# Gate and up projections of a two-layer encoder as 2x2 block products with seven half-size products, one Trainium2 core

## The chip, the cores and the metric

The kernel runs on one core of one Trainium2 chip. The metric is the device time of one execution in microseconds (us); lower is better. The engines are TensorE (PE, with its weight loads as PEld), VectorE (DVE), ScalarE (ACT), GpSimd (POOL) and SyncE (SP), which issues all transfers from HBM.

## What is computed

Two layers, each of a token mixer and a SwiGLU channel mixer, over 512 frames of width 1024, and a final norm. The change touches the channel mixer alone:

```python
h2 = rms_norm(x, norm2_g[l])
x = x + (jax.nn.silu(h2 @ w_gate[l]) * (h2 @ w_up[l])) @ w_down[l]
```

with `w_gate` and `w_up` of 1024 x 2816 and `w_down` of 2816 x 1024, all float32.

## The kernel before

Everything is kept transposed: features lie on the 128 partitions, the 512 frames along the free dimension. A matrix block is 128 x 128 of weights against 128 x 512 of activations. To hold float32 accuracy each operand is split in a high part `hi` (a cast to float32r, on ACT) and a rest `lo` (the difference, on POOL or DVE), and each block product is three matmuls, hi·hi, hi·lo and lo·hi, issued by `mm3` (L327; the matmuls are L332 to L334).

Weights come in units. `loader` (L353) issues one transfer per unit, mostly 128 x 1024 numbers (four blocks of the contraction by two blocks of output columns, 512 KB), into one of four `raw` buffers. `halves` (L365) then makes the `hi` with one cast of 1024 numbers per partition (L368) and the `lo` with two subtractions of 512 (L373), into four `hi` and four `lo` buffers of 1024. A projection (`project`, L566) takes two units, 8 blocks of the contraction and 2 blocks (a pair) of 128 output columns, hence 8·2·3 = 48 matmuls of 512 columns into two banks of PSUM.

The channel mixer (`mixer`, L973) runs over 11 pairs, for each a gate projection and then an up projection, 22 projections in a layer. The right operand is `x` times the norm's gain, split once per layer by `norm_input` (L479); the norm's factor per frame (`nm2.rows`, from `norm_rstd`, L524) is multiplied in afterwards. After a gate projection each of the two 128 x 512 results goes through a multiplication by the rows (DVE), Silu (ACT) and another multiplication by the rows (POOL); after an up projection through a multiplication by the gate's result (DVE), a cast (ACT) and a subtraction (DVE, `split_lo`). `down` (L1006) then runs four projections over all 22 blocks of the activations; in the last layer the fourth is done in two halves of 256 frames.

No order of instructions is written by hand. Each piece is a generator that yields operations, and `Weave` (L60 on) plans them: it holds a clock per engine, a cost per operation, the buffers that are free, and one clock for the access that POOL and DVE share when both operands lie in SBUF. In `run` (L172) it takes the operation that can start first and, among those on the same engine that can start within a short horizon, the one of lowest rank. An operation with two possible engines goes to the one where it would end first; for DVE 2 us are added in that choice (`SHUN`), so that work goes to POOL unless it is far behind. What it picks is the program's order on each engine; every engine then works its queue in that order. Buffers for 128 x 512 results, `row()`, come from a pool of 66 that the planner does not count.

## Time and profile before

| | |
|---|---|
| median of 3 runs | 1153.08 us (1150.91 to 1153.38) |
| profiled execution, its own time | 1153.68 us |
| its span | 1151.2 us |
| PE, matmuls | 1139.3 us busy, 99%, 5306 recorded |
| DVE | 447.7 us busy, 39% |
| ACT | 403.9 us busy, 35% |
| POOL | 750.4 us busy, 65% |
| granted TensorE clock, mean | 0.997 of full speed |

A matmul's duration on the page is longer than the distance to the next one, because they are pipelined: the rate is read from the starts. The profiled execution is 2.5 us longer than its span, and 0.6 us above the median of the runs.

### The profile page before, as it was taken

The numbers are of one execution on the slowest core, as the hardware profiler recorded it, in microseconds if no ns is written. First come the engines' busy times: TensorE is split into PE (matmuls) and PEld (weight loads), VectorE is DVE, ScalarE is ACT, GpSimd is POOL, SyncE is SP. The second block draws the span as 40 slices with busy tenths as digits, with TensorE's granted clock in tenths as the row PEclk, the third lists the DMA queues.
The fourth block names the chain that finished last, engine by engine and source line by source line (L and its number), as shares of the span: only waits on it lengthen the run. The fifth ranks groups of instructions, "written<-read, shape, count | busy, mean of one in ns | idle before, by whom it ended". The sixth has DMA issues, their size and how long they took to land.

```text
span 1151.2 us, 13848 instructions
## 1 busy us (share of the span) xinstructions
PE 1139.3 (99%) x5306; PEld 953.4 (83%) x5306; DVE 447.7 (39%) x766; ACT 403.9 (35%) x531; POOL 750.4 (65%) x583
## 2 busy tenths in 40 slices
PE   8999999999999999999999999999999999999997
PEld 7888888888888888888888888888888888888897
DVE  4899873322222222111059997442222222210003
ACT  6324545332332323222232346452323323322241
POOL 5877977756655655555577699785655665654572
PEclk9999999999999999999999999999999999999999
DMA  9433122333333332323333312233333333323332
GB/s 283 114 105 92 37 78 87 92 110 92 92 105 97 110 100 93 122 98 99 97 103 97 94 60 67 70 112 94 92 94 103 96 92 97 105 83 101 101 121 82
DMA packets 118483, 114.11 MB, mean 99 GB/s; under 512 B 4113, under 2 KB 113809, under 8 KB 118417
## 3 DMA queue, kind: packets, MB, share of 16 engines
q1 hardware_dynamic: 118416, 113.23, 32.5%
q8 instruction: 41, 0.67, 0.2%
q14 instruction: 26, 0.20, 0.1%
HBM read 111.12 MB, written 2.10 MB: 98 GB/s over the span
## 4 chain that ended last, share of the span: by engine, by line
PE 80%; DVE 16%; DMA 1%; issue 1%; ACT 1%; POOL 0%; SPq 0%; DVEq 0%; ACTq 0%; POOLq 0%
PE acc L332 25%; PE acc L333 25%; PE acc L334 25%; DVE conv L308 11%; DVE big L301 4%; PE acc L459 1%; DVE big L308 1%; DMA x<-in_x_t 1%; PE acc L425 1%; PE conv L332 1%; PE conv L334 1%; PE conv L333 1%; DMA raw<-in_w_in 0%; ACT big L284 0%; DVE vmean L727 0%
## 5 line engine op out<-in xcount | busy, mean ns | idle before, releaser
L373 POOL TENSOR_TENSOR lo<-raw,hi 128x512 fp32r<-128x512 f32 x403 | 529.0, 1330 | 330.4 <-ACT hi L368 325.6
L332 PE MATMUL acc<-big,hi 128*128 128x512 f32 (+1 forms) x1516 | 584.2, 385 | 0.5 <-ACT big L284 0.4
L333 PE MATMUL acc<-big,hi 128*128 128x512 f32 (+1 forms) x1516 | 581.4, 383 | 0.3 <-DVE big L308 0.3
L334 PE MATMUL acc<-big,lo 128*128 128x512 f32 (+1 forms) x1516 | 581.2, 383 | 0.0
L368 ACT ACTIVATE hi<-raw 128x1024 fp32r<-128x1024 f32 (+1 forms) x208 | 214.6, 1033 | 506.8 <-PE acc L333 433.7
L333 PEld LDWEIGHTS acc<-big,hi 128*128 128x128 f32 x1516 | 285.4, 188 | 56.4 <-DVE big L308 1.1
L332 PEld LDWEIGHTS acc<-big,hi 128*128 128x128 f32 x1516 | 285.3, 188 | 56.3 <-ACT big L284 1.0
L334 PEld LDWEIGHTS acc<-big,lo 128*128 128x128 f32 x1516 | 285.3, 188 | 56.2
L301 DVE TENSOR_TENSOR big<-acc,big 128x512 f32<-128x512 f32 (+2 forms) x200 | 128.8, 656 | 356.9 <-PE acc L334 343.6
L301 POOL TENSOR_TENSOR big<-big,big 128x512 f32<-128x512 f32 (+2 forms) x176 | 227.6, 1306 | 50.5 <-ACT big L284 38.5
L284 ACT ACTIVATE big<-big 128x512 fp32r<-128x512 f32 (+2 forms) x176 | 106.8, 616 | 158.4 <-DVE big L301 136.3
L308 DVE SCALAR_TENSOR_TENSOR conv<-big,small,conv 128x482 f32<-128x482 f32 (+25 forms) x232 | 156.0, 729 | 4.0 <-ACT conv L284 2.9
L301 DVE TENSOR_TENSOR x<-acc,x 128x512 f32<-128x512 f32 (+1 forms) x30 | 19.6, 654 | 245.5 <-PE acc L334 245.4
L301 DVE TENSOR_TENSOR big<-big,big 128x512 fp32r<-128x512 f32 (+1 forms) x54 | 54.0, 1002 | 32.4 <-ACT big L284 32.4
L308 DVE SCALAR_TENSOR_TENSOR big<-x,small,big 128x512 fp32r<-128x512 f32 x32 | 32.8, 1036 | 18.9 <-ACT big L284 18.9
L284 ACT ACTIVATE big<-x,small 128x512 fp32r<-128x512 f32 (+1 forms) x48 | 29.8, 643 | 20.6 <-DVE x L301 19.1
L284 ACT ACTIVATE big<-x 128x512 f32<-128x512 f32 (+1 forms) x41 | 24.2, 597 | 14.6 <-DVE x L301 14.6
L332 PE MATMUL acc<-hi,big 128*128 128x512 f32 x64 | 24.9, 389 | 0.0
L333 PE MATMUL acc<-lo,big 128*128 128x512 f32 x64 | 24.9, 389 | 0.0
L334 PE MATMUL acc<-hi,big 128*128 128x512 f32 x64 | 24.9, 389 | 0.0
L332 PE MATMUL acc<-big,big 128*128 128x512 f32 (+1 forms) x64 | 21.4, 334 | 2.2 <-DVE y L308 1.4
L333 PE MATMUL acc<-big,big 128*128 128x512 f32 (+1 forms) x64 | 20.6, 322 | 0.0
(55 smaller groups left out, 333.7 us busy)
## 6 DMA issues: line engine op xcount, KB each, us to landing
raw<-in_w_down SPq DMA_DIRECT2D x45, 512.0 KB, 3.4
raw<-in_w_gate SPq DMA_DIRECT2D x44, 512.0 KB, 3.8
raw<-in_w_up SPq DMA_DIRECT2D x44, 512.0 KB, 3.8
raw<-in_w_in SPq DMA_DIRECT2D x32, 512.0 KB, 3.7
raw<-in_w_out SPq DMA_DIRECT2D x16, 512.0 KB, 3.4
raw<-in_w_in SPq DMA_DIRECT2D x28, 256.0 KB, 3.3
raw<-in_w_down SPq DMA_DIRECT2D x9, 256.0 KB, 2.6
x<-in_x_t SPq DMA_DIRECT2D x8, 256.0 KB, 4.5
```

The lines of the kernel that those rows point to most:

```text
L284: ACT.activation(out=t if out is None else out, in_=in_, func=func, **kw)
L301: name, cost, lambda eng=eng: eng.tensor_tensor(out=out, in0=in0, in1=in1, op=op),
L308: [("DVE", cost, lambda: DVE.scalar_tensor_tensor(out=out, in0=in0, scalar=scalar, in1=in1, op0=op0, op1=op1))],
L332: PE.matmul(o, lh, rh, start=start, stop=False)
L333: PE.matmul(o, lh, rl, start=False, stop=False)
L334: PE.matmul(o, ll, rh, start=False, stop=stop)
L368: lambda t: ACT.activation(out=t[:, 0:n], in_=raw[:, 0:n], func=AF.Copy))],
L373: engines[eng].tensor_tensor(out=t[:, a:b], in0=raw[:, a:b], in1=hi[:, a:b].bitcast(F32), op=ALU.subtract)
L425: PE.matmul(o[:, i:i + 1], src[:, t * P:(t + 1) * P], over[n], start=first and i == 0, stop=last and i == len(blocks) - 1, skip_group_chec ...
L459: PE.matmul(ps[:, t * P:(t + 1) * P], cols[:, t:t + 1].broadcast_to([P, P]), ident, start=True, stop=True,)
```

## The change

The first two pairs of each layer (`PLAIN = 2`) stay as they are. For the other nine, each projection is seen as a 2x2 block product: the weights A (1024 x 256) are cut in two halves of the contraction and two blocks of output columns, the normed input B in the same halves of the contraction and two halves of 256 frames. In place of eight half-size products there are seven, of sums and differences of the blocks (`winograd`). Each is 4 blocks of the contraction by three matmuls of 256 columns, 12 matmuls; a projection has 84 of 256 columns where it had 48 of 512.

- **Left factors** (`factors`): from a projection's two `raw` buffers, four sums S1 to S4 of 128 x 512 (`sums`), and then for each of A11, S1, S2, A12, S3, S4, A22 a cast (ACT) and a subtraction of 512. Both may go to POOL or DVE, without the 2 us for DVE (`shun` 0.0). Plain units too are now cast in pieces of 512. There are 11 `hi` and 11 `lo` buffers of 512 in place of four and four of 1024.
- **Right factors** (`right_factors`), once per layer, planned beside the plain pairs: for each of four k, the two halves' `x` times gain times rows (DVE), four sums of 256, and the splits of B11 (256), T1|T2, B21|B22 and T3|N4 (512 each); they stay in 28 rows until the last product. The row pool has 60 buffers in place of 66.
- **Banks.** The seven products use three banks X, Y, Z of 256 columns: X takes A11·B11, then S2·T2, S3·T3 and A22·N4 on top; Y takes S1·T1 and S4·B22; Z takes A12·B21. Between the steps the partial sums are read off: three copies on ACT (p1, p5, u2) and three additions on DVE (c11, c22, c12), each of 256 columns. A product that goes on adding to a bank waits until the sum in it has been read.
- **After them**, a gate's result goes through Silu alone (one of 512, two of 256, ACT); the up's is multiplied by it (one of 512, two of 256). The multiplications by the rows are gone. The splits of these 18 activations (cast and subtraction) are put off until the layer's last such product has been issued, that is beside the first `down`.

```diff
+HALVES = 11
+PLAIN = 2
...
-    big = ctx.enter_context(tc.tile_pool(name="big", bufs=66))
+    big = ctx.enter_context(tc.tile_pool(name="big", bufs=60))
...
-    wv.pool("hi", 4, lambda: named(wts, [P, 1024], F32R, "hi"))
-    wv.pool("lo", 4, lambda: named(wts, [P, 1024], F32R, "lo"))
+    wv.pool("sum", 2, lambda: named(wts, [P, 1024], F32, "sum", 2))
+    wv.pool("hi", HALVES, lambda: named(wts, [P, SEQ], F32R, "hi", HALVES))
+    wv.pool("lo", HALVES, lambda: named(wts, [P, SEQ], F32R, "lo", HALVES))
...
+    def halves(u, raw, n):
+        his = []
+        for a in range(0, n, SEQ):
+            src = raw[:, a:a + SEQ]
+            his.append((src, (yield cast(src, [raw]))))
+        for src, hi in his:
+            lo = yield rest_of(src, hi, [raw])
+            u.hi_t.append(hi)
+            u.lo_t.append(lo)
...
+    def factors(f, rank):
+
+        r0, r1 = f.raws
+        v0, v1 = (r.rearrange("p (a b) -> p a b", a=4) for r in f.raws)
+        a11, a21 = v0[:, :, 0:P], v0[:, :, P:2 * P]
+        a12, a22 = v1[:, :, 0:P], v1[:, :, P:2 * P]
+        src = {"A11": (a11, [r0]), "A12": (a12, [r1]), "A22": (a22, [r1])}
...
+            t = yield add(None, a21, a22, ALU.add, [r0, r1], ("sum", 1))
+            slots.append(t)
+            s1, s2 = (shaped(t[:, i * SEQ:(i + 1) * SEQ], a11) for i in range(2))
+            src["S1"] = s1, [t]
+            yield add(s2, s1, a11, ALU.subtract, [t, r0])
+            src["S2"] = s2, [t]
+            t = yield add(None, a11, a21, ALU.subtract, [r0], ("sum", 1))
+            slots.append(t)
+            s3, s4 = (shaped(t[:, i * SEQ:(i + 1) * SEQ], a11) for i in range(2))
+            src["S3"] = s3, [t]
+            yield add(s4, a12, s2, ALU.subtract, [slots[0], r1])
+            src["S4"] = s4, [t]
...
+        def factor(i, name):
+            yield lambda: turn[0] == i and name in src
+            a, reads = src[name]
+
+            def issue(t):
+                ACT.activation(out=shaped(t, a), in_=a, func=AF.Copy)
+
+            hi = yield Op([("ACT", 0.05 + 0.00094 * SEQ, issue)], reads, [], ("hi", 1))
+            turn[0] += 1
+            lo = yield rest_of(a, hi, reads, 0.0)
+            f.q[name] = hi, lo
...
+        fast_left = [2 * (KF // 2 - PLAIN)]
+        right = {n: [None] * 4 for n in ("B11", "T1", "T2", "B21", "T3", "B22", "N4")}
...
+            def prepare(k):
+                xa, xb, t, d = row(), row(), row(), row()
+                for x, m in ((xa, k), (xb, k + 4)):
+                    yield stt(x, xs[m], scol(l, S_N2 + m), nm2.rows, ALU.mult, ALU.mult)
+                if k % 2 == 0:
+                    pairs[k // 2] = row(F32R), row(F32R)
+                c = h1 if k % 2 else h0
+                ah, al = (a[:, c] for a in pairs[k // 2])
+                yield act(ah, xa[:, h0], AF.Copy)
+                yield split_lo(al, xa[:, h0], ah, "POOL/DVE", 0.0)
+                right["B11"][k] = ah, al
+                yield tt(t[:, h0], xa[:, h1], xa[:, h0], ALU.subtract, "POOL/DVE", 0.0)
+                yield tt(t[:, h1], xb[:, h1], t[:, h0], ALU.subtract, "POOL/DVE", 0.0)
+                yield tt(d[:, h0], xb[:, h1], xa[:, h1], ALU.subtract, "POOL/DVE", 0.0)
+                yield tt(d[:, h1], xb[:, h0], t[:, h1], ALU.subtract, "POOL/DVE", 0.0)
+                for x, n0, n1 in ((t, "T1", "T2"), (xb, "B21", "B22"), (d, "T3", "N4")):
+                    hi, lo = row(F32R), row(F32R)
+                    yield act(hi, x, AF.Copy)
+                    yield split_lo(lo, x, hi, "POOL/DVE", 0.0)
+                    right[n0][k] = hi[:, h0], lo[:, h0]
+                    right[n1][k] = hi[:, h1], lo[:, h1]
+
+            for k in range(4):
+                wv.spawn(prepare(k), base + 10.0 * 2 * PLAIN - 15.0 + 0.01 * k)
...
+            def add(out, x, name, last):
+                yield tt(out, banks[x][:, h0], out, ALU.add)
+                if last:
+                    wv.free("acc", banks[x])
+                done.add(name)
...
+                steps = (
+                    ("A11", "B11", "X", None, lambda: copy(a[:, h0], "X", "p1")),
+                    ("S1", "T1", "Y", None, lambda: copy(b[:, h1], "Y", "p5")),
+                    ("S2", "T2", "X", "p1", lambda: copy(a[:, h1], "X", "u2")),
+                    ("A12", "B21", "Z", None, lambda: add(a[:, h0], "Z", "c11", True)),
+                    ("S3", "T3", "X", "u2", lambda: add(b[:, h1], "X", "c22", False)),
+                    ("S4", "B22", "Y", "p5", lambda: add(a[:, h1], "Y", "c12", True)),
+                    ("A22", "N4", "X", "c22", None),
+                )
...
+                for n, (ln, rn, x, need, then) in enumerate(steps):
+                    yield lambda: ln in f.q
+                    lh, ll = f.q[ln]
+                    yield lambda: need is None or need in done
+                    names = [] if need is None else [
+                        f"{need}_of_{(b if need == 'p5' else a).tensor.name}"]
+                    if need == "c22":
+                        names = [b]
+                    for k in range(4):
+                        yield lambda: right[rn][k] is not None
+                        c = slice(k * P, (k + 1) * P)
+                        m = (lh[:, c], ll[:, c]) + right[rn][k]
+                        if x not in banks:
+                            banks[x] = yield mm3(
+                                None, *m, True, False, ("acc", 1), lambda p: p[:, h0], loose=True,
+                            )
+                        else:
+                            yield mm3(banks[x][:, h0], *m, False, k == 3, after=names, loose=True)
+                    wv.free("hi", lh)
+                    wv.free("lo", ll)
+                    if then:
+                        wv.spawn(then(), r + 1 + 0.1 * n)
+                    else:
+                        done.add("c21")
+                fast_left[0] -= 1
...
+            def gated(a, b, banks, done):
+                def one(need, part, out, src):
+                    yield lambda: need <= done
+                    yield act(out, src(), AF.Silu)
...
+                wv.spawn(one({"c11", "c12"}, "t0", a, lambda: a), 0.0)
+                wv.spawn(one({"c22"}, "c22", b[:, h1], lambda: b[:, h1]), 0.0)
+                wv.spawn(one({"c21"}, "c21", b[:, h0], lambda: banks["X"][:, h0]), 0.0)
...
+                    yield tt(out, src(), by(), ALU.mult, on, 0.0)
...
+                def split(t, x, need):
+                    yield lambda: need <= parts and not fast_left[0]
+                    hi, lo = row(F32R), row(F32R)
+                    yield act(hi, x, AF.Copy)
+                    yield split_lo(lo, x, hi, "POOL/DVE", 0.0)
+                    acts[2 * i + t] = hi, lo
+
+                for t, x, need in ((0, a, {"t0"}), (1, b, {"c22", "c21"})):
+                    wv.spawn(split(t, x, need), base + 10.0 * KF - 12.0 + 0.1 * i)
...
+            winograd(w_gate[l], i, gated)
+            winograd(w_up[l], i, lifted)
...
+        base = 10.0 * len(mains)
+        side.append((len(mains), right_factors, base))
         for i in range(KF // 2):
-            mixer(i)
+            if i < PLAIN:
+                mixer(i)
+            else:
+                fast_mixer(i)
```

**What moves on DVE, in the nine later pairs.** Before, one pair had six rows on DVE (the names: `acc` is PSUM, `big` a row of 128 x 512 in SBUF):

```order
L301 TENSOR_TENSOR big_455_2335<-acc_448_2283,big_445_2263 128x512 [waits PE_49,Pool_49]
L301 TENSOR_TENSOR big_457_2342<-big_455_2335,big_456_2341 128x512 [waits Activation_49]
L301 TENSOR_TENSOR big_459_2356<-acc_449_2284,big_447_2282 128x512 [waits PE_49,Pool_49]
L301 TENSOR_TENSOR big_464_2366<-big_459_2356,big_463_2365 128x512 [waits Activation_49]
L301 TENSOR_TENSOR big_469_2411<-acc_460_2357,big_421_2122 128x512 [waits PE_49]
L301 TENSOR_TENSOR big_471_2430<-acc_461_2358,big_421_2122 128x512 [waits PE_49]
```

Now, in the middle of layer 0's nine pairs, from the end of one up projection (`big_638`, `big_639` are its results, `acc_822`, `acc_832` and `acc_826` its banks X, Z and Y) into the factors of the next projections:

```order
L412 TENSOR_TENSOR lo_831_3900<-sum_819_3839,hi_830_3891 128x512 [waits PE_49,Activation_49]
L412 TENSOR_TENSOR lo_834_3918<-sum_819_3839,hi_833_3909 128x512 [waits PE_49,Activation_49]
L329 TENSOR_TENSOR big_638_2810<-acc_832_3905,big_638_2810 128x256 [waits PE_49]
L412 TENSOR_TENSOR lo_836_3935<-raw_792_3674,hi_835_3926 128x512 [waits Activation_49]
L329 TENSOR_TENSOR big_639_2811<-acc_822_3848,big_639_2811 128x256 [waits PE_49]
L329 TENSOR_TENSOR big_639_2811<-big_639_2811,big_592_2575 128x256 [waits DVE_49]
L457 TENSOR_TENSOR sum_840_3957<-raw_814_3801,raw_815_3810 128x512 [waits DMAHW4_49]
L329 TENSOR_TENSOR big_638_2810<-acc_826_3868,big_638_2810 128x256 [waits PE_49]
L329 TENSOR_TENSOR big_638_2810<-big_638_2810,big_591_2574 128x512 [waits DVE_49]
L457 TENSOR_TENSOR sum_840_3957<-sum_840_3957,raw_814_3801 128x512
L329 TENSOR_TENSOR big_639_2811<-acc_822_3848,big_592_2575 128x256 [waits PE_49]
L457 TENSOR_TENSOR sum_844_3992<-raw_814_3801 128x512
```

The subtractions for `lo`, which were POOL's (L373), and the sums stand on DVE, 11 to a projection, and the additions that read the banks stand between them. POOL has no row left in this stretch but three of the `sum` rows.

**What the first product waits for on DVE.** In layer 0, the last right factor (`big_598`) and then the left factors of the first projection of the new kind (before, DVE had at this place only the rows of the plain pairs, six to a pair, as shown above):

```order
L329 TENSOR_TENSOR big_598_2587<-big_527_2278,big_597_2586 128x512 [waits PE_49,Activation_49]
L412 TENSOR_TENSOR lo_599_2599<-sum_508_2253,hi_549_2370 128x512
L412 TENSOR_TENSOR lo_600_2602<-sum_508_2253,hi_552_2378 128x512
L412 TENSOR_TENSOR lo_602_2611<-raw_503_2224,hi_561_2422 128x512
L412 TENSOR_TENSOR lo_603_2616<-sum_536_2311,hi_564_2432 128x512
L412 TENSOR_TENSOR lo_604_2625<-sum_536_2311,hi_571_2473 128x512
L412 TENSOR_TENSOR lo_605_2633<-raw_503_2224,hi_576_2486 128x512
L329 TENSOR_TENSOR big_588_2551<-acc_574_2479,big_565_2446 128x512 [waits PE_49,Pool_49]
L329 TENSOR_TENSOR big_608_2642<-big_588_2551,big_607_2641 128x512 [waits Activation_49]
```

Six of the seven `lo` of the first new projection stand behind all right factors, and the multiplication that ends pair 1 (`big_588`) stands behind them.

**A hand-over of a bank on PE.** The end of S4·B22 (bank Y, `acc_868`) and the start of A22·N4 (bank X, `acc_864`):

```order
L362 MATMUL acc_868_4136<-big_584_2530,hi_854_4043 128x256
L363 MATMUL acc_868_4136<-big_585_2531,hi_854_4043 128x256
L364 MATMUL acc_868_4136<-big_584_2530,lo_855_4052 128x256
L362 MATMUL acc_868_4136<-big_594_2578,hi_854_4043 128x256
L363 MATMUL acc_868_4136<-big_595_2579,hi_854_4043 128x256
L364 MATMUL acc_868_4136<-big_594_2578,lo_855_4052 128x256
L362 MATMUL acc_864_4116<-big_562_2425,hi_856_4060 128x256 [waits DVE_49]
L363 MATMUL acc_864_4116<-big_563_2426,hi_856_4060 128x256
L364 MATMUL acc_864_4116<-big_562_2425,lo_857_4069 128x256
```

The first matmul of A22·N4 waits for DVE's addition c22, which reads X after S3·T3; the product S4·B22, 12 matmuls, stands between. S2·T2, S3·T3 and S4·B22 wait in the same way for copies on ACT, each with one product between.

## Rows read from the trace of the kernel before

**Rows 1.** The page: busy time by engine; TensorE's granted clock in 40 slices.

```profile
PE 1139.3 (99%) x5306; PEld 953.4 (83%) x5306; DVE 447.7 (39%) x766; ACT 403.9 (35%) x531; POOL 750.4 (65%) x583
PEclk9999999999999999999999999999999999999999
```

**Rows 2.** The page: the chain that ended last, by engine.

```profile
PE 80%; DVE 16%; DMA 1%; issue 1%; ACT 1%; POOL 0%; SPq 0%; DVEq 0%; ACTq 0%; POOLq 0%
```

**Rows 3.** TensorE in order of time, 1094 to 1112 us: start, duration, instruction.

```profile
1094.64 0.39 PE L332 MATMUL acc<-big,hi 128*128 128x512 f32 x1
...
1105.30 0.39 PE L334 MATMUL acc<-big,lo 128*128 128x512 f32 x1
1105.53 0.28 PE L332 MATMUL acc<-big,hi 128*128 128x256 f32 x1
...
1111.28 0.28 PE L332 MATMUL acc<-big,hi 128*128 128x256 f32 x1
```

**Rows 4.** Groups by line and form, DVE, ACT, POOL: count, busy us, mean ns, idle before.

```profile
L301 DVE TENSOR_TENSOR big<-acc,big 128x512 f32<-128x512 f32 x144 | 99.0, 690 | 356.5 <-PE acc L334 343.6 <-ACT big L284 9.7 <-PE acc L459 2.4
L301 DVE TENSOR_TENSOR big<-big,big 128x512 fp32r<-128x512 f32 x44 | 45.2, 1026 | 32.0 <-ACT big L284 32.0
L301 DVE TENSOR_TENSOR big<-acc,big 128x256 f32<-128x256 f32 x8 | 3.3, 413 | 0.0
L368 ACT ACTIVATE hi<-raw 128x512 fp32r<-128x512 f32 x13 | 8.2, 633 | 36.5 <-PE acc L333 30.4 <-PE acc L334 4.0 <-DMA raw<-in_w_in 1.8
L284 ACT ACTIVATE big<-big 128x512 f32<-128x512 f32 x68 | 42.5, 626 | 64.3 <-DVE big L301 64.2
L284 ACT ACTIVATE big<-x,small 128x256 f32<-128x256 f32 x16 | 7.1, 494 | 0.0
L284 ACT ACTIVATE big<-big 128x256 fp32r<-128x256 f32 x8 | 3.3, 410 | 0.6 <-DVE big L301 0.5
L373 POOL TENSOR_TENSOR lo<-raw,hi 128x512 fp32r<-128x512 f32 x403 | 529.0, 1330 | 330.4 <-ACT hi L368 325.6 <-issue 3.7 <-POOL big L301 0.6
```

**Rows 5.** Busy us of each engine (instructions) in two stretches, clock, DMA share, GB/s.

```profile
224.20:256.90 32.70, 32.70 (x146) 27.07 (x145) 7.50 (x10) 10.45 (x13) 20.71 (x16) 1.00 0.33 93
256.90:452.80 195.90, 195.90 (x866) 162.22 (x865) 43.41 (x55) 58.91 (x72) 118.26 (x90) 1.00 0.33 99
```

**Rows 6.** DVE in order of time, first mixers of layer 0, then the last.

```profile
224.22 1.32 DVE L301 TENSOR_TENSOR big<-acc,big 128x512 f32<-128x512 f32 x2 [4.20 <-PE acc L334]
233.08 0.69 DVE L301 TENSOR_TENSOR big<-acc,big 128x512 f32<-128x512 f32 x1 [7.54 <-PE acc L334]
234.47 0.69 DVE L301 TENSOR_TENSOR big<-big,big 128x512 fp32r<-128x512 f32 x1 [0.70 <-ACT big L284]
...
257.56 0.69 DVE L301 TENSOR_TENSOR big<-acc,big 128x512 f32<-128x512 f32 x1 [0.64 <-PE acc L334]
259.01 1.36 DVE L301 TENSOR_TENSOR big<-big,big 128x512 fp32r<-128x512 f32 x1 [0.76 <-ACT big L284]
...
453.40 0.69 DVE L301 TENSOR_TENSOR big<-acc,big 128x512 f32<-128x512 f32 x1 [0.64 <-PE acc L334]
```

**Rows 7.** POOL in order of time, 253 to 262 us.

```profile
253.10 2.55 POOL L373 TENSOR_TENSOR lo<-raw,hi 128x512 fp32r<-128x512 f32 x2 [1.66 <-ACT hi L368]
258.54 2.98 POOL L373 TENSOR_TENSOR lo<-raw,hi 128x512 fp32r<-128x512 f32 x2 [2.89 <-ACT hi L368]
```

**Rows 8.** The chain in order of time: start, length, what (pieces on DVE, one on ACT).

```profile
18.83 1.06 ACT hi L368
...
48.04 8.91 DVE conv L308 x14
...
593.47 0.74 DVE conv L308
594.23 0.74 DVE conv L308
```

**Rows 9.** The page: DMA issues, KB each, median us to landing.

```profile
raw<-in_w_gate SPq DMA_DIRECT2D x44, 512.0 KB, 3.8
```

186 lines of the change are left out of this document (138 added, 48 removed).

## Prediction

> **What bounds the kernel now.** I start with the page: TensorE (PE) is busy for 99% of the span at a full granted clock in all 40 slices [rows 1], and 80% of the chain that ended last is PE's [rows 2]. A busy PE can still be slow inside, so the next view is PE in order of time [rows 3]. From 1094.64 to 1105.53 us stand 48 matmuls of 512 columns: 10.89/48 = 0.2269 us from one to the next. From 1105.53 to 1111.28, where the last `down` goes over to half the frames, stand 48 of 256 columns: 5.75/48 = 0.1198 us. The reader is to see that half the columns cost 53% of the time, not 50%: each matmul carries some 13 ns beside its columns (0.2269 less twice the 0.1071 that the 256 more columns add). Then the mixers themselves: DVE's last multiplications of pairs 1 and 10 stand at 257.56 and 453.40 [rows 6], 195.84 us for 18 projections, 10.88 each, which is 48 x 0.2269: no gap. In that stretch DVE works 43.4 of 195.9 us, ACT 58.9 and POOL 118.3 [rows 5]. So any matmul time that is taken away comes off the end, as long as the other engines, which get more to do, keep up.
>
> **The change part by part.**
>
> *Matmuls.* 36 projections (18 in each layer) go from 48 x 0.2269 = 10.89 us to 84 x 0.1198 = 10.06 us: 0.83 us each, **29.8 us** in all. Seven eighths of the columns alone would be 12.5%; the 13 ns on 36 more matmuls take it down to 7.6%. The Trainium skill (TensorE: Matmul & The Clock Gate, Back-to-back issue gap) gives an isolated gap of columns/2.4 ns plus 2.5; by that I estimate 215.8 and 109.2 ns and a saving of 42.7 us in place of 29.8. The trace differs for both shapes, so the measured distances decide.
>
> *DVE in the nine pairs.* The order puts 23 instructions of 512 columns on DVE per pair (twice 4 sums and 7 `lo`, one multiplication) and 8 of 256 (six additions that read banks, two multiplications). Alone, one of 512 takes 0.69 us [rows 6] and one of 256 from PSUM 0.41 [rows 4]. Two that don't depend on each other overlap a little: two additions in 1.32 us [rows 6], 14 convolution steps in 8.91, 0.64 each [rows 8]. So a pair costs DVE between 23 x 0.63 + 8 x 0.35 = 17.3 us and 23 x 0.69 + 8 x 0.41 = 19.2, beside 2 x 10.06 = 20.1 of PE. It was 43.4/9 = 4.8 per pair [rows 5]. This fits, with 5 to 14% to spare. The slow way that a DVE instruction has, 1.36 us in place of 0.69 when POOL reads SBUF beside it [rows 6, 7] (and POOL's own two `lo` take 2.98 in place of 2.55), is gone here, since POOL has nearly nothing left. I price it at 0 and keep up to +12 us for the range (below).
>
> *ACT in the nine pairs.* 14 casts of 512 at 0.633, six copies and two Silu of 256 at 0.494 at most, one Silu at 0.626 [rows 4]: 13.4 of 20.1 us. Hidden; it is DVE that fills up first.
>
> *Buffers.* A cast takes a `hi` slot when the eleventh-last factor's product has ended, and its own product comes 9 to 10 products of 1.44 us (12 x 0.1198) later, some 13 us. A transfer takes 3.8 us from issue to landing [rows 9], cast and subtraction 0.63 + 0.69: hidden behind that lead. The 60 rows hold what lives at the end of the nine pairs (28 right, 8 plain, 20 of results): 0. The bytes from HBM are the same.
>
> *Hand-overs.* A product that adds to a bank waits for the read of it, with one product of 1.44 us between. c22 needs about 0.1 us from PE's end to DVE's start, 0.41, and as much to get back: 0.6. One instruction of 0.69 ahead on DVE still fits. 0.
>
> *From the plain pairs to the new ones.* Here the cover is thin. The norm's rows are there at 224.2, when DVE's first multiplication starts [rows 6], and pair 1 ends by 257.5; the first product that needs a sum (S1) is due one product later, at 258.9. DVE's queue first has five instructions and then the up multiplication of pair 0, which comes at 233.08 as before [rows 6]. From there to S1's `lo` the order has 29 instructions of 512 and 19 of 256: 29 x 0.63 + 19 x 0.35 = 24.9 us to 29 x 0.69 + 19 x 0.41 = 27.8, and five to seven POOL instructions stand beside them, each of which can cost DVE 0.67 us more (1.36 less 0.69): 0 to 4.7. So S1's `lo` ends at 258.0 to 265.6, 0 to 6.7 us late. Behind it DVE is still in arrears: S1 of the second projection comes after 16 more instructions, about 10 us, where PE asks for it after 8.6: 1 us more. I take **+4 us** per layer, the middle, **+8** in all; bounds 0 and +15.
>
> *From the new pairs to `down`.* 18 casts and subtractions now stand there. PE needs the first of them after four plain blocks, 4 x 6 x 0.2269 = 5.4 us, and then one every 1.36; DVE gives one every 0.69, at worst 1.36 beside POOL. Hidden.
>
> *The start.* The first cast of the program lies on the chain, 1.06 us for 1024 columns [rows 8]; a piece of 512 takes 0.633: up to 0.4 us gained, taken as 0.
>
> Sum, against the profiled execution: 1153.7 - 29.8 + 8 = 1131.9; the median of the runs is 0.6 lower, so I forecast **1131 us**.
>
> **The rivals.**
>
> *DVE sets the pace.* 19.2 us per pair leaves 0.9 over 31 instructions, 0.03 us each. Between convolution steps that wait for each other the distance is 0.77 for 0.74 of work [rows 8], just that. If waits for ACT's casts in line make it 0.05 or 0.06 more than the bare duration, a pair takes 20.8 to 21.1 and 18 pairs give back 12 to 18 us: 1143 to 1149, still faster. For it: 20 of 31 instructions wait for another engine. Against: the lead of 13 us lets most waits be over before they are reached, and then neighbours overlap. The Trainium skill (VectorE: DVE Perf Modes, The DRAIN you can't avoid) says that an instruction can't issue until the one before has left the pipe; that would put DVE at its upper price. The trace has 0.64 where one alone takes 0.74 [rows 8].
>
> *The hand-overs come late (slower).* If DVE or ACT has two instructions ahead of the read, it ends at 0.1 + 2 x 0.69 + 0.41 + 0.1 = 2.0 us, 0.55 after it is due. There are four to a projection, 144 in all: 79 us, 1131 + 79 = 1210. It decides from 0.15 us mean on (22/144), from where the change is slower than before. For it: both engines work in order, and casts that wait for slots stand between the reads. Against: the slot of the cast just ahead comes free a product earlier, and additions stand in the order where PE ends their product.
>
> *The saving doesn't reach the end.* PE's gaps grow as much as its work shrinks, at the two transitions (11 us a layer in place of 4, and some in the pairs): within 0.2% of 1153. For it speaks only that both thin covers, DVE's 5% and the transition, would have to fail at once.
>
> *The fixed part shrinks.* If 5 ns of the 13 went away in a run of 84 equal shapes, 36 x 84 x 0.005 = 15 us more would be gained: 1116. No row shows it; 48 equal ones keep the 13 ns.
>
> **How the numbers follow.** The forecast, 1123 (no stall) to 1139: 0.64. DVE's pace, 1139 to 1150: 0.15. Late hand-overs: 0.11, of which 0.01 still ends within 0.2%. No gain: 0.04. Fixed part smaller, or no stall at all: 0.06. Faster by over 0.2%, which is about what a measurement of this kernel can tell from no change: 0.64 + 0.15 + 0.06 = 0.85; within: 0.05; slower: 0.10. The range leaves out the far ends of both: 1121 to 1146, some 8 in 10.
>
> **What would show it.** Right: the nine pairs of a layer take 181 us in place of 195.8, with matmuls 0.1198 apart; PE waits a few us for DVE at the first products of each layer and nearly nowhere else; DVE is busy 85 to 95% in the pairs, POOL idle. DVE's pace would show as PE waiting for `lo` all along the pairs; late hand-overs as PE waiting for copies or additions 1.4 us after each product. A distance other than 0.12 us would make the first term wrong.

## The result and the profile after

The changed kernel takes **1132.17 us**, median of 4 runs (1130.51 to 1133.65), beside 1153.01 us (1150.91 to 1153.38) for the kernel before on the same chip: ratio 0.9823, 95% interval 0.9804 to 0.9842, 20.8 us faster. The forecast was 1131 us, from 1121 to 1146. The profiled execution took 1130.51 us, the shortest of the four, its span 1128.7.

The page of the changed kernel, busy time by engine, TensorE's granted clock and the chain that ended last (they answer to [rows 1, 2]):

```profile
PE 1110.7 (98%) x6602; PEld 990.5 (88%) x6602; DVE 743.5 (66%) x1324; ACT 548.3 (49%) x992; POOL 541.1 (48%) x411
...
PEclk9999999999999999999999999999999999999999
...
PE 84%; DVE 11%; DMA 1%; ACT 1%; issue 1%; POOL 0%; SPq 0%; DVEq 0%; ACTq 0%; POOLq 0%
```

DVE went from 39 to 66%, POOL from 65 to 48%, and PE is still the engine that sets the end. The next view is PE in order of time, from the first to the last matmul of the nine pairs of layer 0 (answers to [rows 3]):

```profile
255.80 0.28 PE L362 MATMUL acc<-big,hi 128*128 128x256 f32 x1
...
300.06 0.28 PE L364 MATMUL acc<-big,lo 128*128 128x256 f32 x1
...
306.18 0.28 PE L364 MATMUL acc<-big,lo 128*128 128x256 f32 x1
...
440.82 0.28 PE L364 MATMUL acc<-big,lo 128*128 128x256 f32 x1
440.94 0.40 PE L362 MATMUL acc<-big,hi 128*128 128x512 f32 x1
```

From 300.06 to 306.18 stand 51 distances: 0.1200 us each. 18 projections of 84 matmuls take 440.94 - 255.80 = 185.14 us, in layer 1 as well; 1512 x 0.1200 would be 181.4. So 3.7 us are lost per layer, where before nothing was. PE's waits (what waited for what: us in total, times, longest), and then its rows in order of time, say where:

```profile
PE acc L364 <- DVE lo L412: 6.0, 4, 2.0
```

```profile
259.65 0.39 PE L364 MATMUL acc<-big,lo 128*128 128x256 f32 x1 [2.01 <-DVE lo L412]
269.52 0.39 PE L364 MATMUL acc<-big,lo 128*128 128x256 f32 x1 [0.98 <-DVE lo L412]
```

Four waits (two per layer, the longest 2.0 us) hold 6.0 us of idle time; counted from matmul start to matmul start they make some 7.0 of the 7.4 lost. They are the two that the prediction named, the S1 products of the first and of the second projection. DVE around them, in order of time (answers to [rows 6]):

```profile
231.59 0.69 DVE L329 TENSOR_TENSOR big<-acc,big 128x512 f32<-128x512 f32 x1 [4.73 <-PE acc L364]
...
258.90 1.29 DVE L412 TENSOR_TENSOR lo<-sum,hi 128x512 fp32r<-128x512 f32 x2
...
262.51 0.69 DVE L329 TENSOR_TENSOR big<-acc,big 128x512 f32<-128x512 f32 x1
...
265.17 0.68 DVE L457 TENSOR_TENSOR sum<-raw,raw 128x512 f32<-128x512 f32 x1
265.77 0.69 DVE L412 TENSOR_TENSOR lo<-raw,hi 128x512 fp32r<-128x512 f32 x1
```

S1's `lo` starts at 258.90. The reader is to see three things: DVE stands idle for 4.73 us ahead of the up multiplication of pair 0; from then on it has hardly a gap; and neighbours of 0.69 us start 0.60 apart. Last, the two layers' pairs by engine (answers to [rows 5]):

```profile
257.00:440.00 183.00, 180.01 (x1497) 179.45 (x1496) 158.05 (x277) 107.12 (x214) 21.67 (x12) 1.00 0.38 112
810.00:993.00 183.00, 180.13 (x1497) 179.76 (x1498) 158.13 (x277) 107.12 (x214) 22.41 (x13) 1.00 0.37 110
```

DVE is busy 158 of 183 us (86%), ACT 107 (59%), POOL 22 (12%).

### The profile page after: what moved, and what is told of

Read it like the earlier page. It is cut to its first block, busy times and chain, and to the rows that moved or that the text cites. A ratio compares the mean times of both kernels' runs of the same rounds, so it can differ in the third digit from the quotient of the medians.

```text
span 1128.7 us, 17495 instructions
## 1 busy us (share of the span) xinstructions
PE 1110.7 (98%) x6602; PEld 990.5 (88%) x6602; DVE 743.5 (66%) x1324; ACT 548.3 (49%) x992; POOL 541.1 (48%) x411
## 4 chain that ended last, share of the span: by engine, by line
PE 84%; DVE 11%; DMA 1%; ACT 1%; issue 1%; POOL 0%; SPq 0%; DVEq 0%; ACTq 0%; POOLq 0%
PE acc L362 27%; PE acc L364 27%; PE acc L363 27%; DVE conv L336 6%; DVE big L329 3%; PE acc L560 1%; ACT big L312 1%; DVE lo L412 1%; DMA x<-in_x_t 1%; PE acc L526 1%; DVE big L336 1%; PE conv L364 1%; PE conv L363 1%; PE conv L362 1%; DMA raw<-in_w_in 1%
## 5 line engine op out<-in xcount | busy, mean ns | idle before, releaser
L364 PE MATMUL acc<-big,lo 128*128 128x256 f32 (+1 forms) x1948 | 642.3, 330 | 6.0 <-DVE lo L412 6.0
L362 PE MATMUL acc<-big,hi 128*128 128x256 f32 (+1 forms) x1948 | 645.2, 331 | 0.5 <-ACT big L312 0.5
L363 PE MATMUL acc<-big,hi 128*128 128x256 f32 (+1 forms) x1948 | 642.0, 330 | 0.5 <-DVE big L336 0.5
L412 POOL TENSOR_TENSOR lo<-raw,hi 128x512 fp32r<-128x512 f32 x259 | 345.3, 1352 | 378.1 <-ACT hi L403 369.2
L363 PEld LDWEIGHTS acc<-big,hi 128*128 128x128 f32 x1948 | 370.4, 190 | 33.8 <-DVE big L336 1.2
L362 PEld LDWEIGHTS acc<-big,hi 128*128 128x128 f32 x1948 | 370.4, 190 | 33.8 <-ACT big L312 0.8
L403 ACT ACTIVATE hi<-raw 128x512 fp32r<-128x512 f32 x259 | 161.0, 629 | 244.9 <-PE acc L363 205.5
L329 DVE TENSOR_TENSOR big<-acc,big 128x256 f32<-128x256 f32 (+4 forms) x254 | 131.1, 530 | 59.0 <-PE acc L364 39.2
L312 ACT ACTIVATE big<-big 128x512 fp32r<-128x512 f32 (+3 forms) x208 | 115.9, 593 | 96.8 <-DVE big L329 63.4
L336 DVE SCALAR_TENSOR_TENSOR conv<-big,small,conv 128x482 f32<-128x482 f32 (+26 forms) x232 | 156.2, 733 | 5.7 <-ACT conv L312 4.7
L412 DVE TENSOR_TENSOR lo<-sum,hi 128x512 fp32r<-128x512 f32 x144 | 97.4, 703 | 17.2 <-ACT hi L481 16.7
L329 DVE TENSOR_TENSOR big<-big,big 128x512 fp32r<-128x512 f32 (+3 forms) x144 | 92.4, 676 | 4.7 <-ACT big L312 2.9
L481 ACT ACTIVATE hi<-raw 128x512 fp32r<-128x512 f32 x108 | 68.1, 631 | 52.8 <-PE acc L363 47.5
L312 ACT ACTIVATE big<-x,small 128x512 fp32r<-128x512 f32 (+1 forms) x48 | 30.4, 649 | 31.8 <-DVE x L329 29.2
```

The costliest lines, as they stand in the source:

```text
L312: ACT.activation(out=t if out is None else out, in_=in_, func=func, **kw)
L329: name, cost, lambda eng=eng: eng.tensor_tensor(out=out, in0=in0, in1=in1, op=op),
L336: [("DVE", cost, lambda: DVE.scalar_tensor_tensor(out=out, in0=in0, scalar=scalar, in1=in1, op0=op0, op1=op1))],
L362: PE.matmul(o, lh, rh, start=start, stop=False, **kw)
L363: PE.matmul(o, lh, rl, start=False, stop=False, **kw)
L364: PE.matmul(o, ll, rh, start=False, stop=stop, **kw)
```

## Experiments

Theory: the gain is the matmuls' alone, and what is given back is a **debt of DVE's time** ahead of the first new projections. Rivals: the waits belong to the first new projections whatever stands ahead of them; the order of a queue makes them; hand-overs, buffers or the side edits matter too. Each set of runs has its own runs of the kernel before, so kernels of different sets are compared by their ratios; "faster than the changed kernel" below divides by 0.9823. An interval is 0.0009 to 0.0021 wide on either side, so differences under some 3 us between sets are not told apart.

### The side edits alone

```diff
-PLAIN = 2
+PLAIN = 11
...
-        side.append((len(mains), right_factors, base))
```

> All eleven pairs are plain, and the right factors are left out; what stays of the change are its side edits: 60 rows of 512 columns, eleven buffers of 512 for casts and subtractions in place of fewer of 1024, and all weights cast in pieces of 512. Theory 1 (the gain is the matmuls' alone, the side edits were priced at 0 to -0.4 us): 1152 to 1154 us, as the kernel before. Rival (the side edits carry part of it, in either direction, through ScalarE's 0.633 for a piece of 512 against 1.06 for 1024, or the shorter lead of the buffers): more than 3 us from 1153, and the term of the matmuls is off by the same amount.

Measured: 1153.22 us, ratio 1.0012 (1.0003 to 1.0021), 1.4 us slower than before. The buffers and the casts of 512 gain nothing and cost 0.3 to 2.4 us: theory 1, with the sign of the small term turned round. So the seven products and all that belongs to them are worth 0.9823/1.0012, some 22 us.

### Three plain pairs

```diff
-PLAIN = 2
+PLAIN = 3
```

> Three plain pairs ahead of the nine become three ahead of eight: the right factors have one pair more of cover. In the changed kernel TensorE loses 2.2 us at the first S1 product of each layer and 1.1 us at the S1 of the second projection, 3.7 us per layer with the small ones. Theory 1 (VectorE's arrears behind the 28 right factors, which run out with time): both waits go, 2 x 3.7 = 7.4 us are won, and 2 x 2 projections lose the 0.83 us that seven products save each, 3.3 us: 4 us faster than the changed kernel, 1128 us, with no wait over 0.3 us at S1. Rival (the wait belongs to whichever projections are the first with seven products, because the sums before S1 form a chain of their own): the waits stay, later by a pair, and only the 3.3 us are lost: 1135.5 us.

Measured: 1136.38 us, ratio 0.9863 (0.9849 to 0.9876), 4.6 us slower than the changed kernel. The number is near the rival's, but neither had the mechanism. The wait at S1 is gone, as the theory said; a new one stands one product later, at the one that adds to the bank of A11·B11 and waits for ACT's copy. PE and then ACT in order of time:

```profile
283.58 0.58 PE L362 MATMUL acc<-big,hi 128*128 128x256 f32 x1 [2.62 <-ACT big L312]
```

```profile
279.51 0.63 ACT L312 ACTIVATE big<-big 128x512 fp32r<-128x512 f32 x1 [6.03 <-DVE big L329]
280.05 0.62 ACT L481 ACTIVATE hi<-sum 128x512 fp32r<-128x512 f32 x1
281.59 0.63 ACT L481 ACTIVATE hi<-sum 128x512 fp32r<-128x512 f32 x1 [0.92 <-DVE sum L457]
282.12 0.61 ACT L312 ACTIVATE big<-big 128x512 fp32r<-128x512 f32 x1
282.65 0.61 ACT L481 ACTIVATE hi<-raw 128x512 fp32r<-128x512 f32 x1
283.17 0.36 ACT L312 ACTIVATE big<-acc 128x256 f32<-128x256 f32 x1
```

A11·B11 had ended by 279.5. Its copy stands at 283.17, behind five casts, of which the first waits for DVE's up multiplication of the last plain pair and another for a DVE sum. DVE's lateness reaches PE by another door: an engine that works in order passes on the wait of whatever stands ahead. And the clock falls after it (last section).

### Using DVE's idle time

```diff
-                    yield stt(x, xs[m], scol(l, S_N2 + m), nm2.rows, ALU.mult, ALU.mult)
+                    op = stt(x, xs[m], scol(l, S_N2 + m), nm2.rows, ALU.mult, ALU.mult)
+                    op.port = ()
+                    yield op
```

> The planner no longer keeps the eight multiplications of the norm (the rows that the right factors start from) off the time in which GpSimd works: on VectorE they now all stand ahead of the up multiplication of pair 0, where its queue waited 4.7 us for TensorE, and the sums of the first projection move up with them. Theory 1 (the arrears come from that idle time of VectorE): the wait at the first S1 (2.2 us) goes and the one at the second projection's S1 (1.1 us) shrinks, 2 to 3.5 us per layer: 1125 to 1128 us against 1132 of the changed kernel. Rival (what is pulled forward runs beside GpSimd's subtractions and gets slow, 1.36 us in place of 0.69 each, so the sums are ready no earlier): 1131 to 1133 us, and the multiplications of the norm show means over 1 us.

Measured: 1139.02 us, ratio 0.9887 (0.9873 to 0.9900), 7.4 us slower than the changed kernel: the theory's number fell. DVE in order of time, then POOL, then PE:

```profile
225.16 7.55 DVE L336 SCALAR_TENSOR_TENSOR big<-x,small,big 128x512 f32<-128x512 f32 x5
...
261.97 0.68 DVE L329 TENSOR_TENSOR big<-acc,big 128x512 f32<-128x512 f32 x1
```

```profile
225.39 3.36 POOL L329 TENSOR_TENSOR big<-big,big 128x512 f32<-128x512 f32 x2 [3.14 <-ACT big L312]
228.72 3.43 POOL L412 TENSOR_TENSOR lo<-raw,hi 128x512 fp32r<-128x512 f32 x2
```

```profile
263.64 0.39 PE L362 MATMUL acc<-big,hi 128*128 128x256 f32 x1 [4.12 <-ACT big L312]
```

Five multiplications beside POOL take 7.55 us, 1.51 each where one alone takes 0.75: the rival was right that the time moved is lost again, though its number, 1131 to 1133, did not come either. The first up multiplication of the last plain pair starts hardly earlier, at 261.97 in place of 262.51. The wait at S1 went, and PE waits 4.12 us for ACT's copy, which stands behind the cast of that multiplication.

### The right factors in the order of their need

```diff
-                for x, n0, n1 in ((t, "T1", "T2"), (xb, "B21", "B22"), (d, "T3", "N4")):
...
+                r = base + 10.0 * 2 * PLAIN - 15.0 + 0.01 * k
+                wv.spawn(split(xb, "B21", "B22"), r + 0.3)
+                wv.spawn(last(), r + 0.4)
+                yield from split(t, "T1", "T2")
```

(`split` makes the cast and the subtraction of one pair of factors, `last` the two sums of `d` and their split.)

> Only the order of VectorE's and ScalarE's work before the first seven-product projection is changed: the splits for T1 and T2 of all four k come first, those for B21 and B22 next, those for T3 and N4 last, as TensorE asks for them, and S1's own subtraction moves up by some 20 instructions, ahead of the late ones. No work is added or removed. Theory A (it is a debt of time: VectorE has more to do by the end of the second projection's sums than it has time, whatever stands first): the wait of 2.2 us at the first S1 goes, the second projection's S1, now due 2.2 us earlier, waits 3.3 us in place of 1.1, and the time stays within 2 us of the changed kernel, 1130 to 1134 us. Rival (it is only the queue's order: S1's subtraction stands behind factors that are not due yet): both waits go or fall under 0.5 us, 2 x 3.3 = 6.6 us faster, about 1125 us.

Measured: 1134.03 us, ratio 0.9845 (0.9828 to 0.9862), 2.5 us slower than the changed kernel, which the noise does not tell from no change. PE's waits in layer 0, in order of time:

```profile
259.36 0.39 PE L362 MATMUL acc<-big,hi 128*128 128x256 f32 x1 [0.47 <-ACT big L312]
267.53 0.38 PE L364 MATMUL acc<-big,lo 128*128 128x256 f32 x1 [1.87 <-DVE lo L412]
270.54 0.39 PE L364 MATMUL acc<-big,lo 128*128 128x256 f32 x1 [1.32 <-DVE lo L412]
```

The 2.0 us at the first S1 are gone and come back at the second projection: 1.87 + 1.32 where 0.98 stood. Waits of 2.99 before and 3.66 now: the debt stays, and the order only chooses who pays. That is theory A; the 6.6 us that the rival expected did not come.

### Less work for POOL beside DVE

```diff
-                yield tt(tg, tg, nm2.rows, ALU.mult, "POOL/DVE")
+                yield tt(tg, tg, nm2.rows, ALU.mult, "DVE")
...
-                yield split_lo(al, xa[:, h0], ah, "POOL/DVE", 0.0)
+                yield split_lo(al, xa[:, h0], ah, "DVE")
...
+                    op.port = ()
```

(and the other operations on the right factors in the same way)

> As with the multiplications of the norm set free of GpSimd's time, and now also what GpSimd has in that stretch is cut: the four multiplications of the gates by the norm's row and all work on the right factors are given to VectorE alone; two subtractions of weights stay on GpSimd. Theory (the waits at the first S1 products are a debt of VectorE's time, 3.3 us per layer, and each GpSimd instruction beside VectorE makes it larger: 1.50 us in place of 0.75 for a multiplication, 1.78 in place of 0.69 for a subtraction): VectorE uses 4.7 us in which it waited, takes over five to six instructions of 0.60, and loses 2 us in place of some 3 to collisions: the debt falls by 2 to 3 us per layer, 1126 to 1129 us. Rival (the multiplications run slow whatever GpSimd does, because they are many in a row): no better than with them set free alone, 1139 us.

> The same, with three plain pairs ahead of the eight. One more plain pair costs 2 x 0.83 us per layer, 3.3 us in all, and gives VectorE 21.8 us of cover, of which it has other work for some 5. Theory (with the collisions gone the debt is paid before the first sum is due, and ScalarE's copies no longer stand behind casts that wait for VectorE): no wait of over 0.5 us at the first products of the layer, 1132 - 7.4 + 3.3 = 1128 us, where three plain pairs alone gave 1136. Rival (ScalarE's copy stays behind casts in its queue): a wait of 2.8 us at the third product remains in each layer, 1134 to 1136 us.

Measured: with two plain pairs 1134.51 us, ratio 0.9838 (0.9823 to 0.9852); with three 1129.76 us, ratio 0.9799 (0.9785 to 0.9814), 2.8 us faster than the changed kernel and 23.4 faster than before. DVE of the version with two plain pairs, then its PE:

```profile
230.51 2.73 DVE L336 SCALAR_TENSOR_TENSOR big<-x,small,big 128x512 f32<-128x512 f32 x4
...
260.21 1.28 DVE L329 TENSOR_TENSOR big<-acc,big 128x512 f32<-128x512 f32 x2
```

```profile
263.00 0.38 PE L362 MATMUL acc<-big,hi 128*128 128x256 f32 x1 [3.46 <-ACT big L312]
```

Four multiplications of the norm in a row, with POOL idle beside them, start 0.68 us apart: they are not slow by themselves, and the rival falls. The last plain pair's first up multiplication comes at 260.21, 2.3 us ahead of the changed kernel's 262.51 (3.0 ahead, counted from the first matmul of the nine pairs, which is at 256.50 here): by that row the debt fell by the 2 to 3 us expected, and S1's wait is gone. The time did not follow, it is above the theory's 1126 to 1129: PE waits 3.46 us for ACT's copy, in the same queue order as above. With three plain pairs the number is near the theory's 1128: the debt is nearly paid, and that wait is small. PE of that version:

```profile
280.78 0.39 PE L362 MATMUL acc<-big,hi 128*128 128x256 f32 x1 [0.77 <-ACT big L312]
```

8 pairs then take 162.3 us, 1 us over 1344 x 0.1200. This is the best version run. Its interval and the changed kernel's (0.9804 to 0.9842) overlap a little, so it is faster than the kernel before for certain, and than the changed kernel probably.

### ACT's copies ahead of the casts

In the version with two plain pairs, the last plain pair's casts are planned only after the first three copies:

```diff
+                yield lambda: i < PLAIN - 1 or len(copied) == 3
                 hi, lo = row(F32R), row(F32R)
                 yield act(hi, tu, AF.Copy)
```

> The version with two plain pairs in which VectorE alone does the gates' multiplications and the right factors, with one thing more: on ScalarE the two casts of the last plain pair, which wait for VectorE's up multiplications, stand behind the first three copies of the first seven-product projection, and no longer ahead of them. No work is added or removed. Theory (what was left there, 3.6 us at the third product and 1.5 us of slow clock behind it in each layer, was ScalarE's queue order alone, and VectorE's debt is paid): no wait of over 0.5 us at the first products, 2 x 5.1 = 10 us faster than that version, 1124 to 1126 us, and so faster than both kernels. Rival (VectorE's debt is still there and shows at the next product that needs it): one wait of 2 us or more at a subtraction or an addition of the first two projections, 1128 to 1134 us.

Measured: 1131.67 us, ratio 0.9830 (0.9816 to 0.9844), within the noise of the changed kernel. The first two copies now come in time. The third does not; PE, then ACT with the second and the third copy:

```profile
264.29 0.38 PE L362 MATMUL acc<-big,hi 128*128 128x256 f32 x1 [2.39 <-ACT big L312]
```

```profile
259.06 0.38 ACT L312 ACTIVATE big<-acc 128x256 f32<-128x256 f32 x1 [0.54 <-PE acc L364]
262.82 0.63 ACT L481 ACTIVATE hi<-sum 128x512 fp32r<-128x512 f32 x1 [3.38 <-DVE sum L457]
...
263.88 0.36 ACT L312 ACTIVATE big<-acc 128x256 f32<-128x256 f32 x1
```

It stands behind a cast of the second projection that waits 3.38 us for a DVE sum. One door was shut and the rest of the debt came through the next: the rival's number, with the wait at a copy and not at a subtraction or an addition. Three plain pairs with this order were not tried.

### How much room DVE has in the pairs

```diff
             yield add(s4, a12, s2, ALU.subtract, [slots[0], r1])
+            for _ in range(2):
+                yield tt(s4, a12, s2, ALU.subtract, "DVE")
```

> Each seven-product projection repeats its last subtraction of 512 columns (the one for S4) twice more on VectorE, writing the same values: four more instructions per pair, 2.4 us at the distance of 0.60 us that the changed kernel's trace shows between neighbours. VectorE was busy 158 of 183 us in the pairs, 17.7 us of the 20.57 that a pair takes, so it would be at 20.1, just under. Theory (VectorE has 2.9 us per pair to spare and nothing else waits for it): the pairs themselves gain no wait; only the second projection's S1 moves by up to 1.2 us per layer: 1132 to 1136 us. Rival (the spare time is not usable, since the queue waits in order for ScalarE and TensorE): each of the 18 pairs gives 1 us or more, 1150 us and over.

> As with four more, but the last subtraction is repeated four times per projection, eight more per pair: 4.8 us more of VectorE, 17.7 + 4.8 = 22.5 us per pair against TensorE's 20.57. Theory (VectorE then sets the pace, and only then): every pair takes 1.9 us longer, 18 x 1.9 = 35 us, 1167 us, with TensorE waiting for subtractions all along the pairs. Rival (the buffers' lead of some 13 us and the idle ends absorb most of it): under 1145 us.

(the second with `range(4)`). Measured: 1156.36 us, ratio 1.0036 (1.0022 to 1.0050), and 1194.61 us, ratio 1.0365 (1.0346 to 1.0384): 24.5 and 62.5 us slower than the changed kernel. A stretch of 150 us in the pairs of the changed kernel, then with four more (columns as in [rows 5]: stretch, its length, PE, PEld, DVE, ACT, POOL, clock, DMA share, GB/s):

```profile
290.00:440.00 150.00, 150.00 (x1251) 149.85 (x1250) 125.97 (x219) 87.75 (x174) 14.74 (x10) 1.00 0.39 115
```

```profile
290.00:440.00 150.00, 145.11 (x1191) 143.28 (x1191) 148.47 (x242) 82.56 (x167) 22.69 (x14) 1.00 0.37 110
```

PE is full in the first and DVE, at 99%, in the second: there DVE sets the pace. In the changed kernel a pair takes 20.16 us (168 x 0.1200) and 16.9 of DVE (125.97/150). With eight more, the same wait of PE stands one pair apart:

```profile
302.89 0.39 PE L362 MATMUL acc<-big,hi 128*128 128x256 f32 x1 [0.45 <-DVE big L329]
...
325.96 0.39 PE L362 MATMUL acc<-big,hi 128*128 128x256 f32 x1 [0.45 <-DVE big L329]
```

A pair takes 23.07 us, 2.9 more where I had 1.9: each repeated subtraction starts 0.03 us after the end of the one before, whose tile it writes again, so they stand 0.72 apart, not 0.60; and one sum per pair now goes to POOL, beside which a subtraction of DVE takes 1.79 us in place of 0.69. That makes 16.9 + 8 x 0.72 - 0.60 + 1.1 = 23.2 us of DVE. 18 x 2.9 = 52, and most of the rest is a larger debt at the start of each layer. With four more I expected 20.1 us of DVE and no loss; from the third pair on a pair takes 20.4 to 22.6 (every 168th matmul), 21.4 on average. The rival's number came, but not for its reason, a queue that waits: DVE stands idle for only 1% of that stretch. It is the planner: seeing DVE fuller, it puts the sum for S1 on POOL in most projections (13 of 18 in layer 0, 3 in the changed kernel). DVE and POOL of that run, in order of time:

```profile
302.82 1.28 DVE L412 TENSOR_TENSOR lo<-sum,hi 128x512 fp32r<-128x512 f32 x2
304.02 0.68 DVE L412 TENSOR_TENSOR lo<-raw,hi 128x512 fp32r<-128x512 f32 x1
304.62 2.39 DVE L412 TENSOR_TENSOR lo<-sum,hi 128x512 fp32r<-128x512 f32 x2
```

```profile
304.24 1.63 POOL L457 TENSOR_TENSOR sum<-raw,raw 128x512 f32<-128x512 f32 x1 [8.55 <-DVE lo L412]
```

Beside it two subtractions take 2.39 us in place of 1.28: moving 0.60 us of work off DVE cost DVE 1.1. Per pair that makes 4 x 0.72 - 2 x 0.60 + 2 x 1.1 = 3.9 us, above the 3.3 (20.2 less 16.9) that DVE has to spare, and 16.9 + 3.9 = 20.8 of the 21.4 that a pair takes. The theory's number fell by that; that DVE sets the pace only once its room is used up is borne out by both runs. The room is 16%, just beyond the 5 to 14% of the prediction.

### Fewer buffers

```diff
-HALVES = 11
+HALVES = 8
```

> Eight buffers for casts and eight for subtractions of weights in place of eleven. The lead of a cast over its product falls from 9 to 10 products of 1.44 us (some 13 us) to 6 or 7 (some 9 us). Theory (the lead only has to cover cast, subtraction and the hand-overs between them, some 2 us and VectorE's queue): within 2 us of the changed kernel, 1130 to 1134 us. Rival (the lead is what lets VectorE catch up after its stretches of adding and multiplying): TensorE waits for subtractions in every pair, by 0.5 us or more, over 1140 us.

Measured: 1133.42 us, ratio 0.9834 (0.9819 to 0.9849), 1.3 us slower than the changed kernel: the theory. From the second pair on a pair takes the same 20.16 us. The waits at the first two projections are longer, by 1.7 us for the nine pairs of a layer (186.81 us in place of 185.14), but in layer 0 those begin 1.1 us earlier (254.67 in place of 255.80): PE reaches the debt sooner and waits longer for it, as far as the rows tell.

### The price of a hand-over

```diff
-    ORDER = ("A11", "S1", "S2", "A12", "S3", "S4", "A22")
+    ORDER = ("A11", "S2", "S1", "A12", "S3", "S4", "A22")
```

and `steps` in the same order.

> The order of the seven products is changed so that the product with S2, which adds to the bank that the first product has just left, comes right behind it: between a product and the addition that has to read its bank no other product stands any more, once per projection, 36 times in all. The result is the same. It prices the hand-over that the prediction called 0.6 us (0.1 to the reader, 0.41 of addition or 0.49 of copy, 0.1 back) and hid behind one product of 1.44 us. Theory 1 (a hand-over costs some 0.6 us when nothing covers it, and waits for what VectorE or ScalarE has in hand, 0.3 us on average): 36 x 0.6 to 0.9 = 22 to 32 us slower than the changed kernel, 1154 to 1164 us, with one gap of 0.6 to 0.9 us per projection in TensorE's row. Rival A (the hand-overs come late, two instructions wait ahead of the read): gaps of 2 us, 72 us slower, over 1200 us. Rival B (TensorE may run on): within 3 us of 1132.

Measured: 1143.50 us, ratio 0.9925 (0.9911 to 0.9938), 11.8 us slower than the changed kernel; none of the three. The order of TensorE explains it: from the fourth projection on, the planner puts the next projection's first product between the two, so most hand-overs kept their cover. The loss lies in the first projections, with waits of 0.5 to 2.9 us. So it had to be forced, with a count that lets a projection start only when the one before is in line:

```diff
+                yield lambda: fast_left[2] == turn
                 a, b = row(), row()
...
                 fast_left[0] -= 1
+                fast_left[2] += 1
```

> Again the product with S2 directly behind the first product, which leaves its bank to it, and now each projection's products may only begin when those of the one before have all been put in line, so that no product of a neighbour can be placed between the two: one hand-over per projection stands uncovered, 36 in all. The result is the same. Theory 1 (an uncovered hand-over costs the copy of 0.36 to 0.39 us and some 0.1 to 0.15 on either side, 0.6 to 0.7, and up to 0.3 more for what ScalarE has in hand): 36 x 0.6 to 1.0 = 22 to 36 us slower than the changed kernel, 1154 to 1168 us. Rival A (two instructions stand ahead of the copy): 2 us each, 72 us, over 1200. Rival B (a hand-over costs nothing even uncovered): 1130 to 1136 us.

Measured: 1182.88 us, ratio 1.0260 (1.0239 to 1.0281), 50 us slower than the changed kernel. PE's waits (engine, what waited for what: us in total, times, longest), one of them in order of time, and ACT there:

```profile
PE acc L362 <- ACT big L312: 30.8, 33, 1.0
PE acc L362 <- DVE big L329: 12.6, 3, 6.3
```

```profile
313.10 0.28 PE L364 MATMUL acc<-big,lo 128*128 128x256 f32 x1
314.40 0.39 PE L362 MATMUL acc<-big,hi 128*128 128x256 f32 x1 [1.02 <-ACT big L312]
```

```profile
313.46 0.61 ACT L481 ACTIVATE hi<-raw 128x512 fp32r<-128x512 f32 x1
313.98 0.36 ACT L312 ACTIVATE big<-acc 128x256 f32<-128x256 f32 x1
```

An uncovered hand-over costs 1.30 - 0.12 = 1.18 us here and 1.03 at the next, in turns; the idle time is 0.93 on average over 33. I had put 0.6 to 1.0: a cast that stands ahead of the copy, here the one at 313.46, adds 0.4 to 0.5 every time. Two to a pair, with the slower first distance behind each, make 2.4 us (a pair takes 22.57 in place of 20.16), 43 us in all; most of the rest is a wait of some 6 us at the second projection of each layer and the lower clock behind it.

## Why the prediction held

- *Matmuls*, -29.8: the distance is 0.1200 in place of 0.1198, so a projection saves 10.89 - 10.08 = 0.81 us and all of them 29.2. The estimate of 42.7 is not what came; nor did the fixed part shrink.
- *DVE in the nine pairs*, 0: right, a little under the lower price of 17.3: DVE works 16.9 us of a pair's 20.16 in the steady stretch, and 17.8 of 20.57 over all nine (158.05/183). The upper price needed instructions that don't overlap. Neighbours start 0.60 apart and last 0.69, which is an overlap. The Trainium skill (VectorE: DVE Perf Modes, The DRAIN you can't avoid) says that the next instruction does not start until the pipe is empty, and adds that one that is not held starts earlier; the prediction took the first half alone, and the 0.60 agrees with the second, if these neighbours count as not held, which no run here tests. POOL, forecast idle, still had 12 instructions in 183 us. The rival on DVE's pace begins 3.3 us further, as the runs with repeated subtractions show.
- *ACT* and *Buffers*, 0: right (107 of 183 us; eight buffers cost 1.3 us, within the noise).
- *Hand-overs*, 0 where a product covers them: right, there is no wait for them in the nine pairs. The 0.6 us were the price with nothing ahead of the read, and the prediction saw room for one instruction of 0.69 more. In the forced run a cast stands ahead each time, and the price is 1.03 or 1.18; 1.44 us of cover hold it with 0.26 to 0.41 to spare. That is for a copy on ACT: an addition on DVE (c22) was not run without cover.
- *From the plain pairs to the new ones*, +8: 2 x 3.7 = 7.4, at the two products named; 3 and 1 us were forecast for them, 2.2 and 1.1 came. The queue had the 29 and 19 instructions of the forecast and took 28.0 us (231.59 to 259.59, the end of S1's `lo`), inside 24.9 to 32.5 and near the middle; both its start and the moment that S1 is due came 1.5 us earlier than in the trace before, which cancels. So the term did not come right by luck. The runs show a debt of DVE's time that order can move but not remove. What I had not seen is the second way out, through ACT's queue.
- *To `down`*, 0: no wait there. *The start*, 0 to -0.4: all side edits together are +1.4 (0.3 to 2.4), the one term whose sign was off. The traces place only 0.4 of it, in the stretches between the pairs of layer 0 and those of layer 1 and behind these; where the rest lies is not shown.

The sum in what was measured: -29.2 + 7.4 + 1.4 = -20.4; the medians differ by 20.8. The two profiled spans differ by more, 22.5. The prediction read a full clock in all 40 slices, but a 9 there is 90% or more: in the first 50 us the kernel before was granted 0.97 on average and the changed one 1.00, and its nine pairs begin 1.5 us earlier (255.80 in place of 257.29). That part is the clock's and no gain of the change.

## What to carry to other kernels

When a product is made cheaper by sums on another engine, two things decided here: that engine's share in the steady state, and its debt where the steady state begins, when the new work is due at once and the old work is not done yet. Reordering its queue only moved that debt, and work that waits in other in-order queues carried it along. More cover alone was slower (one more plain pair, 4.6 us), and sparing DVE the collisions alone gained nothing; both together paid most of it. And a helper engine on the same memory is no help if it slows the first one by more than it takes over, as the sums on POOL did (1.1 us for 0.60).

## What the runs showed of the hardware

- DVE and POOL on SBUF operands slow each other, and which of the two pays differs. With four more subtractions a sum took POOL 1.63 us and DVE's neighbour 1.79 in place of 0.69. In the changed kernel the six such sums on POOL took 3.25 us on average (POOL spans are rough); beside four of them DVE's instructions of 512 kept 0.69 to 0.81, beside the other two one took 1.46 or 1.48. The group on the page of the changed kernel, and DVE beside the first of the six, which lasts from 270.15 to 273.64:

```profile
L457 POOL TENSOR_TENSOR sum<-raw,raw 128x512 f32<-128x512 f32 x6 | 19.5, 3252 | 76.7 <-DVE lo L412 76.7
```

```profile
270.58 1.29 DVE L412 TENSOR_TENSOR lo<-sum,hi 128x512 fp32r<-128x512 f32 x2
```

- TensorE's clock. After waits of 2.01 and 0.98 us in the changed kernel it stays at full speed. After the 4.12 us of the run that used DVE's idle time it does not. A window of that run, then the windows behind the first wait of each layer in the run with four more subtractions, 3.01 and 3.03 us:

```profile
264.00:267.50 3.50, 3.50 (x19) 3.50 (x18) 3.50 (x7) 1.86 (x4) 0.00 (x0) 0.52 0.35 121
```

```profile
261.50:265.00 3.50, 3.50 (x29) 3.50 (x30) 3.50 (x6) 1.29 (x3) 0.00 (x0) 1.00 0.00 0
826.30:829.80 3.50, 3.45 (x16) 3.45 (x17) 3.50 (x6) 0.91 (x2) 0.00 (x0) 0.52 0.00 0
```

A granted clock of 0.52 is the lower level, 1.2 GHz: some 16 matmuls stand 0.213 apart in place of 0.120, 1.5 us on top of the wait. The same came after waits of 2.62 and 3.46 us in other runs. The wait's length alone does not decide it: with the right factors in the order of their need the clock fell after 1.89 us in layer 1 (0.50 granted) and not after 1.87 in layer 0, and in the run with four more subtractions it stayed at 1.00 behind 3.01 us and fell to 0.52 behind 3.03. What else decides is left open.
